# A two-layer hybrid encoder on one core: the rotary key's column tile with low parts in its second half

## Chip, cores and metric

The kernel runs on 1 core of a Trainium2 chip. The metric is the device time of one execution in microseconds (us). Before the change it is 918.32 us, the median of 3 runs (918.1 to 919.2).

## What is computed

Two encoder layers over 256 positions of 1024 features. Each layer normalizes x, makes one combined projection, runs three mixing branches, merges them through gates, and then runs a SwiGLU block and an embedding block. The change is in the combined projection; the rest is cut.

```python
h = rms_norm(x, norm_mix_pre[i])
z = h @ w_in[i]
c_q, c_kv, k_rope, q_c, k_c, v_c, g_a, g_b, g_c = jnp.split(z, split_points, axis=-1)
o_a = mla_attention(c_q, c_kv, k_rope, positions, ...)   # k_r = apply_rope(k_rope, positions), 32 columns, all heads
o_b = fourier_mix(h)
o_c = windowed_gqa(q_c, k_c, v_c, positions, gqa_sink[i])
```

## The kernel before

**Products.** Features lie on partitions, the 256 positions along the free axis. All weights come as tiles of 128 by 128, eight to a chunk, 279 chunks in the order of use. SyncE loads a chunk (512 KB) into one of three staging buffers `w`. ScalarE writes the rounded high part `wh` (line 175) and VectorE the low part `wl` (w minus wh, line 180), each with three buffers of its own. x is split in the same way into `XH` and `XL`. A product of a weight tile and an x tile is then three matmuls of 256 columns on TensorE: high by high, low by high, high by low.

**Order.** The program is written out by a planner (class `Order`) with a clock of its own: each part is a generator that is resumed when the planner thinks its inputs are ready. The orders of TensorE, ScalarE and VectorE are exactly the orders in which the planner issues; GpSimd and SyncE are ordered by the framework. So a change of the planner's clock at one place moves instructions on three engines behind it. Each engine works strictly in its order and waits at the first instruction whose inputs are late.

**The first projection of a layer** (`k_outer`, lines 371 to 395, called at line 893). Four pairs of column tiles `z1` are accumulated at once: three query latents, the key latent, the rotary key, the window keys, the window values and the first window queries. For each of the first six contraction tiles k (one chunk each) there are three passes of eight matmuls, all on line 385: `wh` by XH, `wl` by XH, `wh` by XL. The last two contraction tiles (`LATE`) come pair by pair through `mains` (lines 357, 358 and 364). In layer 0 this loop is interleaved with the norm of x: VectorE sums squares into `acc_npre_first`, TensorE reduces them over partitions (`ss_pre_first`, line 486), VectorE makes the mean (`ms_pre_first`), GpSimd the power of minus one half (`rt_pre_first`, line 497), and TensorE spreads it to rows (`pr_pre_first`, line 503).

**The rotary key** is the tile `kr`, column pair 2, column 0. Its 128 columns are the 32 rope columns, the same 32 with halves swapped, and both once more. After the projection the result `zk` is scaled by the norm (line 285), multiplied with cosines and sines `KC`, and one f32 matmul with the constant `sel` (line 844, `pkL`) adds row m and row 32+m and repeats the sum over 128 partitions.

**GpSimd** fills constants, computes the position differences `di` (two int32 subtractions, line 682, for the distance table that VectorE starts at line 687 with `df`), the small powers, and two sums of squares for the latents (line 824).

**After the projection**: `zq12` and `zq3` (window queries), the latents' norm (`ss_lat`, `ms_lat`, `rt_lat`, `pr_lat`), scores of the first window head `sc`, and the Fourier products `pu`, which multiply with a table `dft` split into `mixH` and `mixL` in the same tile as other operands.

Of the kernel before, what the change touches and what calls it, by code (L numbers as in the profile page):

```python
# [9 lines left out]
F32 = mybir.dt.float32  # L10
# [7 lines left out]
P = 128  # L18
# [8 lines left out]
KT = D_MODEL // P  # L27
# [4 lines left out]
T_MM = 0.109  # L32
# [9 lines left out]
LATE = (2, 2, 2)  # L42
CT = 8
# [30 lines left out]
def r128(k):  # L74
    return np.arange(k * P, (k + 1) * P)
# [146 lines left out]
def encoder(ctx: ExitStack, tc: tile.TileContext, order, gxT, pT, pos, cst, dftT, mask, sink, wts, outT):  # L222
    nc = tc.nc
    V, S, G, T = nc.vector, nc.scalar, nc.gpsimd, nc.tensor

    one = ctx.enter_context(tc.tile_pool(name="one", bufs=1))
# [16 lines left out]
    O = Order()  # L243
# [8 lines left out]
    def take(tag, name, shape=(P, 2, SEQ), dt=None):  # L252
        pool, n, d = pools[tag]
        while min(slots[tag]) > O.now:
            yield min(min(slots[tag]), O.now + 0.2)
        q = min(range(n), key=lambda q: slots[tag][q])
        slots[tag][q] = 1e9
        t = pool.tile(list(shape), dt or d, tag=tag, name=name, bufs=n)
        held.append((t, tag, q))
        return t  # L260
# [7 lines left out]
    def line(gen):  # L268

        try:  # L270
            while True:
                O.wait(next(gen))
        except StopIteration as e:
            return e.value
# [33 lines left out]
    def have(key):  # L308

        O.until(lambda: key in rd)  # L310
        O.wait(rd[key])

    ws = Weights(nc, O, stage, high, wts, order)
# [12 lines left out]
    def weights(n=1):  # L326
        O.until(lambda: ws.ready(n) < 1e8)
        O.wait(ws.ready(n))

    def step():  # L330
        ws.flush()
        O.step()

    def mains(ps, keys, rhs, start=True, stop=True, skip=False, there=None):

        i = 0
        while i < len(keys):
            O.until(lambda: ws.ready(high=True) < 1e8)
            O.wait(ws.ready(high=True))
            c, pos = divmod(len(order), CT)  # L340
            group = range(i, min(i + CT - pos, len(keys)))
            w = {}
            ws.use(c, 1)
            for j in group:
                if there and there(j):
                    have(there(j))

            c1, pos = divmod(len(order), CT)
            if c1 != c:
                ws.use(c, -1)  # L350
                continue
            group = range(i, min(i + CT - pos, len(keys)))
            for j in group:
                w[j] = ws.get(keys[j])
            for j in group:
                rh, rl = rhs(j)
                T.matmul(ps, w[j][0], rh, start=start and j == 0, stop=False, skip_group_check=skip)  # L357
                T.matmul(ps, w[j][0], rl, start=False, stop=False, skip_group_check=skip)  # L358
                O.spend(2 * T_MM)
                step()  # L360
            O.until(lambda: ws.at[c] < 1e8)
            O.wait(ws.at[c])
            for j in group:
                T.matmul(ps, w[j][1], rhs(j)[0], start=False, stop=stop and j == len(keys) - 1, skip_group_check=skip)  # L364
                O.spend(T_MM)
                O.step()
            ws.use(c, -1)
            step()
            i = group[-1] + 1

    def k_outer(pairs, key, rhs, done, late):


        for k in range(KT - late):
            have(("x", k))
            if k == 0:
                weights(2 * len(pairs))
                keep_warm(None)
            weights(2 * len(pairs))
            w = [[ws.get(key(k, n, c)) for c in range(2)] for n in range(len(pairs))]  # L380
            xh, xl = rhs(k)
            for part, mov in ((0, xh), (1, xh), (0, xl)):
                for n in range(len(pairs)):
                    for c in range(2):
                        T.matmul(pairs[n][:, c, :], w[n][c][part], mov, start=(k == 0 and c == 0 and part == 0 and mov is xh),  # L385
                                 stop=False, skip_group_check=True)
                        O.spend(T_MM)
                    if n % 3 == 2:
                        O.step()
            ws.flush()  # L390
        for n in range(len(pairs)):
            ks = range(KT - late, KT)
            for c in range(2):
                mains(pairs[n][:, c, :], [key(k, n, c) for k in ks], lambda q: rhs(ks[q]), start=False, skip=True,
                      there=lambda q: ("x", ks[q]))
            done(n)

    zeros = one.tile([P, SEQ], BF16, tag="zeros", name="zeros")
# [3 lines left out]
    def keep_warm(step):  # L402

        if step is None:
            O.warm = None
            return
        pw = ppo.tile([P, SEQ], F32, tag="po", name=f"warm{O.now:.0f}", bufs=1)
        idle[0] = 0.0

        def warm(us):  # L410
            idle[0] += us
            while idle[0] > step:
                idle[0] -= step
                T.matmul(pw, zeros[:, :P], zeros, start=True, stop=True)

        O.warm = warm
# [1 line left out]

    gx = one.tile([P, C_ALL + KT * SEQ], F32, tag="gx", name="gx")
    gs, x = gx[:, :C_ALL], gx[:, C_ALL:].rearrange("p (j t) -> p j t", t=SEQ)  # L420
    ones = one.tile([P, P], F32, tag="ones", name="ones")
    G.memset(ones, 1.0)
    mhalf = one.tile([P, 4], F32, tag="mhalf", name="mhalf")
    G.memset(mhalf, -0.5)
# [304 lines left out]
    def win(i, k, cols):  # L729
        return ("w_in", i, r128(k), cols)  # L730
# [20 lines left out]
    for i in range(DEPTH):  # L751
# [16 lines left out]
        g1 = [[cq[0], cq[1]], [cq[2], cq[3]], [kr, kc_cols], [vc_cols, qc_cols[0]]]  # L768
        z1 = [line(take("mm" if n < 3 else "s", f"z1{L}_{n}")) for n in range(4)]
# [114 lines left out]
        def fourier_tables():  # L884
            for n, at in enumerate((OC + 2, OA, OA + 2)):
# [4 lines left out]
                rd["dft", n] = yield from split_to(at, 2, f)  # L890
                drop(f, rd["dft", n])

        k_outer(z1, lambda k, n, c: win(i, k, g1[n][c]), xr, lambda n: None, LATE[0])
        O.start(latents())
        O.start(fourier_tables())
        O.start(window_vq0(z1[3]))
# [436 lines left out]

        first = [line(take("mm" if q < 3 else "s", f"ff{L}_{q}")) for q in range(4)]
        k_outer(first, lambda k, n, c: (wgu[c], i, r128(k), r128(n)), xr, lambda n: O.start(swiglu(first[n], n)), LATE[1])
        for j in range(4, FT):
            ps = line(take("mm" if j % 2 else "s", f"ff{L}_{j}"))
# [36 lines left out]

        pg = [line(take("mm", f"pg{L}_{q}")) for q in range(3)]
        k_outer(pg, lambda k, n, c: ("w_ple_gate", i, r128(k), r128(2 * n + c)), xr, lambda n: O.start(gated(pg[n], n)), LATE[2])
        last = i == DEPTH - 1
        for c in range(2):
# [80 lines left out]
```

## Time and profile before

| | |
|---|---|
| median of 3 runs | 918.32 us (918.1 to 919.2) |
| the profiled execution | 919.09 us |
| its span in the trace | 917.2 us |
| TensorE busy, matmuls | 897.5 us (98%), 7497 |
| VectorE, ScalarE busy | 690.5 us (75%), 546.9 us (60%) |
| GpSimd busy, instructions | 34.5 us (4%), 50 |
| chain that ended last | TensorE 90%, issue 4%, VectorE 2%, GpSimd 2% |

The span runs from the first to the last instruction in the trace; 1.9 us of the execution lie around it. A matmul's busy time is longer than the distance to the next one, as matmuls are pipelined: the distance is what a matmul costs when many follow each other.

### The profile page before, as it was taken

How to read it: one execution, taken by the hardware profiler on the slowest of the kernel's cores; microseconds unless marked ns; L12 is line 12 of the kernel's file. 1: busy time of each engine (PE TensorE's matmuls, PEld its weight loads, DVE VectorE, ACT ScalarE, POOL GpSimd, SP SyncE). 2: the span in 40 equal slices, each digit the busy share in tenths (PEclk: the TensorE clock that was granted, in tenths of full speed). 3: DMA queues.
4: the chain of work that ended last, by engine and by line, in shares of the span. 5: the costliest groups of instructions: out<-in, count | busy, mean ns of one | idle time of the engine just before them, and what ended most of it. 6: DMA issues, size and time to landing. Idle time of an engine off the chain costs nothing.

```text
span 917.2 us, 18357 instructions
## 1 busy us (share of the span) xinstructions
PE 897.5 (98%) x7497; PEld 890.2 (97%) x7497; DVE 690.5 (75%) x1066; ACT 546.9 (60%) x937; POOL 34.5 (4%) x50
## 2 busy tenths in 40 slices
PE   8999999999999999999999999999999999999995
PEld 7999999999999999999999999999999999999995
DVE  6899888786887777445789998887858877764475
ACT  6688667645654445444657786776556545544444
POOL 2200000000000000000002000000000000000001
PEclk9999999999999999999999999999999999999998
DMA  7632544555556556554554344544655566555551
GB/s 255 188 123 82 172 160 139 165 173 182 169 168 211 185 185 185 184 184 138 171 156 145 105 138 133 178 157 146 199 178 171 179 190 188 187 174 177 184 163 69
DMA packets 43845, 152.25 MB, mean 166 GB/s; under 512 B 5232, under 2 KB 6000, under 8 KB 43760
## 3 DMA queue, kind: packets, MB, share of 16 engines
q1 hardware_dynamic: 43760, 151.07, 52.3%
q8 instruction: 59, 0.97, 0.4%
q14 instruction: 26, 0.21, 0.1%
HBM read 150.00 MB, written 1.05 MB: 165 GB/s over the span
## 4 chain that ended last, share of the span: by engine, by line
PE 90%; issue 4%; DVE 2%; POOL 2%; DMA 1%; ACT 0%; SPq 0%; DVEq 0%; POOLq 0%; ACTq 0%
PE ffL L364 8%; PE ffL L358 8%; PE ffL L357 8%; PE gpL L364 5%; PE ofL L364 5%; PE ofL L358 5%; PE ofL L357 5%; PE gpL L358 5%; PE gpL L357 5%; PE ffL L385 4%; PE brL L364 3%; PE brL L358 3%; PE brL L357 3%; PE z1L L385 2%; PE omL L364 2%
## 5 line engine op out<-in xcount | busy, mean ns | idle before, releaser
L180 DVE TENSOR_TENSOR wl<-w,wh 128x1024 fp32r<-128x1024 f32 (+1 forms) x280 | 339.9, 1218 | 92.1 <-ACT wh L175 91.5
L175 ACT ACTIVATE wh<-w 128x1024 fp32r<-128x1024 f32 (+1 forms) x280 | 293.8, 1054 | 192.8 <-PE ofL L358 49.6
L357 PE MATMUL ffL<-xs_mixL,wh 128*128 128x256 f32 x608 | 148.4, 281 | 0.0
L358 PE MATMUL ffL<-xs_mixL,wh 128*128 128x256 f32 x608 | 148.2, 281 | 0.0
L357 PEld LDWEIGHTS ffL<-xs_mixL,wh 128*128 128x128 f32 x608 | 114.7, 189 | 0.0
L358 PEld LDWEIGHTS ffL<-xs_mixL,wh 128*128 128x128 f32 x608 | 114.7, 189 | 0.0
L358 PE MATMUL ofL<-hidL,wh 128*128 128x256 f32 x352 | 87.0, 283 | 0.0
L357 PE MATMUL ofL<-hidH,wh 128*128 128x256 f32 x352 | 87.0, 283 | 0.0
L364 PE MATMUL ffL<-xs_mixL,wl 128*128 128x256 f32 x608 | 86.6, 281 | 0.0
L364 PEld LDWEIGHTS ffL<-xs_mixL,wl 128*128 128x128 f32 x608 | 78.3, 189 | 0.0
L358 PEld LDWEIGHTS ofL<-hidL,wh 128*128 128x128 f32 x352 | 67.0, 190 | 0.0
L357 PEld LDWEIGHTS ofL<-hidH,wh 128*128 128x128 f32 x352 | 67.0, 190 | 0.0
L357 PE MATMUL brL<-mixH,wh 128*128 128x256 f32 x256 | 64.1, 283 | 0.0
L358 PE MATMUL brL<-mixL,wh 128*128 128x256 f32 x256 | 64.0, 283 | 0.0
L285 DVE TENSOR_TENSOR fzL<-ffL,R_pre_mixL 128x512 f32<-128x512 f32 x44 | 30.0, 689 | 32.8 <-PE ffL L364 32.5
L364 PE MATMUL ofL<-hidH,wl 128*128 128x256 f32 x352 | 52.2, 284 | 0.0
L358 PEld LDWEIGHTS brL<-mixL,wh 128*128 128x128 f32 x256 | 49.0, 191 | 0.0
L357 PEld LDWEIGHTS brL<-mixH,wh 128*128 128x128 f32 x256 | 49.0, 191 | 0.0
L357 PE MATMUL gpL<-xs_pleL,wh 128*128 128x256 f32 x192 | 48.3, 284 | 0.0
L357 PE MATMUL gpL<-xs_first,wh 128*128 128x256 f32 x192 | 48.0, 283 | 0.0
L358 PE MATMUL gpL<-xs_pleL,wh 128*128 128x256 f32 x192 | 47.7, 281 | 0.0
L358 PE MATMUL gpL<-xs_first,wh 128*128 128x256 f32 x192 | 47.4, 280 | 0.0
(429 smaller groups left out, 2030.1 us busy)
## 6 DMA issues: line engine op xcount, KB each, us to landing
w<-wts SPq DMA_DIRECT2D x278, 512.0 KB, 3.5
dftL<-dft SPq DMA_DIRECT2D x6, 256.0 KB, 3.9
gx<-gx SPq DMA_DIRECT2D x3, 256.0 KB, 5.5
outT<-gx SPq DMA_DIRECT2D x3, 256.0 KB, 2.3
w<-wts SPq DMA_DIRECT2D x2, 256.0 KB, 3.3
p<-pT SPq DMA_DIRECT2D x2, 256.0 KB, 3.8
dist<-mask SPq DMA_DIRECT2D x1, 256.0 KB, 6.4
outT<-gx SPq DMA_DIRECT2D x2, 128.0 KB, 2.4
```

The costliest lines, as they stand in the source:

```text
L175: self.nc.scalar.activation(h[:, s], w[:, s], AF.Copy)
L180: self.nc.vector.tensor_tensor(out=l[:, s], in0=w[:, s], in1=h[:, s], op=ALU.subtract)
L285: V.tensor_tensor(out=out, in0=a, in1=b, op=op)
L357: T.matmul(ps, w[j][0], rh, start=start and j == 0, stop=False, skip_group_check=skip)
L358: T.matmul(ps, w[j][0], rl, start=False, stop=False, skip_group_check=skip)
L364: T.matmul(ps, w[j][1], rhs(j)[0], start=False, stop=stop and j == len(keys) - 1, skip_group_check=skip)
L385: T.matmul(pairs[n][:, c, :], w[n][c][part], mov, start=(k == 0 and c == 0 and part == 0 and mov is xh), stop=False, skip_group_check=True)
```

## The change

The second half of the rotary key's high tile, columns 64 to 127, is overwritten by a GpSimd copy with the low parts of the same weights (the two halves held the same columns). One matmul of that tile by XH then gives high by high in rows 0 to 63 and low by high in rows 64 to 127; one by XL adds high by low (and low by low). So the tile takes two matmuls for a contraction tile in place of three, 16 fewer in all. The constant `sel` now adds four rows, m, 32+m, 64+m and 96+m. The two matmuls stand in the third pass; in the late part the tile's four matmuls come behind those of the window keys. The copies are 8 a layer, each behind the split of its chunk. The constant `ones` shrinks from 128 columns to 1.

```diff
--- before.py
+++ after.py
@@ -368,7 +368,12 @@
             step()
             i = group[-1] + 1
 
-    def k_outer(pairs, key, rhs, done, late):
+    def beside(w):
+
+        G.tensor_copy(w[0][:, 64:], w[1][:, 64:])
+        O.run("pool", 0.3)
+
+    def k_outer(pairs, key, rhs, done, late, twin=None):
 
 
         for k in range(KT - late):
@@ -378,11 +383,19 @@
                 keep_warm(None)
             weights(2 * len(pairs))
             w = [[ws.get(key(k, n, c)) for c in range(2)] for n in range(len(pairs))]
+            if twin:
+                beside(w[twin[0]][twin[1]])
             xh, xl = rhs(k)
-            for part, mov in ((0, xh), (1, xh), (0, xl)):
+            for q, (part, mov) in enumerate(((0, xh), (1, xh), (0, xl))):
                 for n in range(len(pairs)):
                     for c in range(2):
-                        T.matmul(pairs[n][:, c, :], w[n][c][part], mov, start=(k == 0 and c == 0 and part == 0 and mov is xh),
+                        if (n, c) == twin:
+                            if q == 2:
+                                for m in (xh, xl):
+                                    T.matmul(pairs[n][:, c, :], w[n][c][0], m, start=False, stop=False, skip_group_check=True)
+                                    O.spend(T_MM)
+                            continue
+                        T.matmul(pairs[n][:, c, :], w[n][c][part], mov, start=(k == 0 and q == 0 and c == (twin == (n, 0))),
                                  stop=False, skip_group_check=True)
                         O.spend(T_MM)
                     if n % 3 == 2:
@@ -390,9 +403,26 @@
             ws.flush()
         for n in range(len(pairs)):
             ks = range(KT - late, KT)
+            tw = []
+            if twin and twin[0] == n:
+                ws.align(2)
+                weights(late)
+                ws.use(len(order) // CT, 1)
+                at = len(order) // CT
+                tw = [ws.get(key(k, *twin)) for k in ks]
+                for w in tw:
+                    beside(w)
             for c in range(2):
-                mains(pairs[n][:, c, :], [key(k, n, c) for k in ks], lambda q: rhs(ks[q]), start=False, skip=True,
-                      there=lambda q: ("x", ks[q]))
+                if not (tw and c == twin[1]):
+                    mains(pairs[n][:, c, :], [key(k, n, c) for k in ks], lambda q: rhs(ks[q]), start=False, skip=True,
+                          there=lambda q: ("x", ks[q]))
+            for k, w in zip(ks, tw):
+                have(("x", k))
+                for q, m in enumerate(rhs(k)):
+                    T.matmul(pairs[n][:, twin[1], :], w[0], m, start=False, stop=(q == 1 and k == KT - 1), skip_group_check=True)
+                    O.spend(T_MM)
+            if tw:
+                ws.use(at, -1)
             done(n)
 
     zeros = one.tile([P, SEQ], BF16, tag="zeros", name="zeros")
@@ -418,7 +448,7 @@
 
     gx = one.tile([P, C_ALL + KT * SEQ], F32, tag="gx", name="gx")
     gs, x = gx[:, :C_ALL], gx[:, C_ALL:].rearrange("p (j t) -> p j t", t=SEQ)
-    ones = one.tile([P, P], F32, tag="ones", name="ones")
+    ones = one.tile([P, 1], F32, tag="ones", name="ones")
     G.memset(ones, 1.0)
     mhalf = one.tile([P, 4], F32, tag="mhalf", name="mhalf")
     G.memset(mhalf, -0.5)
@@ -890,7 +920,7 @@
                 rd["dft", n] = yield from split_to(at, 2, f)
                 drop(f, rd["dft", n])
 
-        k_outer(z1, lambda k, n, c: win(i, k, g1[n][c]), xr, lambda n: None, LATE[0])
+        k_outer(z1, lambda k, n, c: win(i, k, g1[n][c]), xr, lambda n: None, LATE[0], (2, 0))
         O.start(latents())
         O.start(fourier_tables())
         O.start(window_vq0(z1[3]))
@@ -1403,8 +1433,7 @@
     cst = np.zeros((P, 2 * P), np.float32)
     cst[:, :P] = np.eye(P, dtype=np.float32)
     for m in range(P):
-        cst[m % 32, P + m] = 1.0
-        cst[32 + m % 32, P + m] = 1.0
+        cst[m % 32::32, P + m] = 1.0
     gns = np.zeros((P, C_ALL), np.float32)
     far = np.abs(np.arange(SEQ)[:, None] - np.arange(SEQ)[None, :]) > WINDOW
     mask = np.ascontiguousarray(np.where(far, np.float32(1e30), np.float32(0)).reshape(2, P, SEQ).transpose(1, 0, 2))
```

**GpSimd, the head of the program** (`wh<-wl` are the new copies, `ISA` is the instruction that stands ahead of `di`). Before:

```order
L1108 MEMSET altL_619 128x512
L682 ISA
L682 TENSOR_TENSOR di<-posr,posc 128x256 x2
L497 TENSOR_TENSOR rt_pre_first<-ms_pre_first,mhalf 128x2
L824 TENSOR_TENSOR s01L_479<-s01L_479 128x256
L824 TENSOR_TENSOR s01L_479<-s01L_479,s23L_480 128x256
L497 TENSOR_TENSOR rt_latL_611<-ms_latL_608,mhalf 128x4
```

Now:

```order
L1138 MEMSET altL_618 128x512
L373 COPY wh_123<-wl_124 128x64
L373 COPY wh_125<-wl_126 128x64
L373 COPY wh_127<-wl_128 128x64
L373 COPY wh_251<-wl_252 128x64
L712 ISA
L712 TENSOR_TENSOR di<-posr,posc 128x256 x2
L373 COPY wh_284<-wl_285 128x64
L527 TENSOR_TENSOR rt_pre_first<-ms_pre_first,mhalf 128x2
L373 COPY wh_323<-wl_324 128x64
L373 COPY wh_401<-wl_402 128x64 x2
L854 TENSOR_TENSOR s01L_476<-s01L_476 128x256
```

Four copies, for contraction tiles 0 to 3, now stand ahead of the ISA instruction and of `di`, the fifth stands behind `di`, the sixth behind `rt_pre_first`.

**TensorE, layer 0, contraction tiles 4 and 5** (`wh_284` and `wl_285` are tile 4, `wh_323` and `wl_324` tile 5). Before:

```order
L385 MATMUL z1L_1_137<-xs_first,wh_284 128x256 x2
L385 MATMUL z1L_2_138<-xs_first,wh_284 128x256 x2
L385 MATMUL z1L_3_139<-xs_first,wh_284 128x256 x2
L385 MATMUL z1L_0_136<-xs_first,wh_323 128x256 x2
L385 MATMUL z1L_1_137<-xs_first,wh_323 128x256 x2
L385 MATMUL z1L_2_138<-xs_first,wh_323 128x256 x2
L385 MATMUL z1L_3_139<-xs_first,wh_323 128x256 x2
L385 MATMUL z1L_0_136<-xs_first,wl_324 128x256 x2
L385 MATMUL z1L_1_137<-xs_first,wl_324 128x256 x2
L385 MATMUL z1L_2_138<-xs_first,wl_324 128x256 x2
L503 MATMUL pr_pre_first<-cs,rt_pre_first 128x128 x2
```

Now:

```order
L516 MATMUL ss_pre_first<-ones,acc_npre_first 128x1 x2
L398 MATMUL z1L_3_139<-xs_first,wl_285 128x256 x2
L398 MATMUL z1L_0_136<-xs_first,wh_284 128x256 x2
L398 MATMUL z1L_1_137<-xs_first,wh_284 128x256 x2
L395 MATMUL z1L_2_138<-xs_first,wh_284 128x256 x2
L398 MATMUL z1L_2_138<-xs_first,wh_284 128x256
L398 MATMUL z1L_3_139<-xs_first,wh_284 128x256 x2
L533 MATMUL pr_pre_first<-cs,rt_pre_first 128x128 x2
L398 MATMUL z1L_0_136<-xs_first,wh_323 128x256 x2
L398 MATMUL z1L_1_137<-xs_first,wh_323 128x256 x2
```

The spreading of the norm, `pr_pre_first`, moved from the second pass of tile 5 to the end of tile 4; the pair of line 395 is the rotary key's.

**VectorE, layer 0, behind the projection** (`ms_lat` is the latents' mean, `mixL<-dftL_0` the low part of the first Fourier table, `zq` the window queries). Before:

```order
L293 TENSOR_SCALAR ms_latL_608<-ss_latL_603 128x2 x2
L285 TENSOR_TENSOR mixL_135<-dftL_0_483,mixH_134 128x512
L180 TENSOR_TENSOR wl_573<-w_472,wh_572 128x1024
L285 TENSOR_TENSOR qcL_140<-zqL_567,qcL_140 64x512 x2
L289 SCALAR_TENSOR_TENSOR zqL_635<-zq3L_569,R_pre_first 128x256
L289 SCALAR_TENSOR_TENSOR sbcL_0_648<-dist,scL_0_625 128x512
```

Now:

```order
L293 TENSOR_SCALAR ms_latL_559<-ss_latL_554 128x2 x2
L285 TENSOR_TENSOR zvsL_529<-z1L_3_139,R_pre_first 128x256
L289 SCALAR_TENSOR_TENSOR zq0L_568<-z1L_3_139,R_pre_first 128x256
L753 TENSOR_SCALAR TT<-KC 64x256 x2
L289 SCALAR_TENSOR_TENSOR zqL_588<-zq12L_482,R_pre_first 128x512
L180 TENSOR_TENSOR wl_575<-w_467,wh_574 128x1024
L285 TENSOR_TENSOR qcL_140<-zq0L_568,qcL_140 64x256 x2
L285 TENSOR_TENSOR vcL_144<-vctL_581,vcL_144 128x2x128
L285 TENSOR_TENSOR qcL_140<-zqL_588,qcL_140 64x512 x2
L289 SCALAR_TENSOR_TENSOR zqL_627<-zq3L_571,R_pre_first 128x256
L285 TENSOR_TENSOR mixL_135<-dftL_0_480,mixH_134 128x512
L289 SCALAR_TENSOR_TENSOR sbcL_0_642<-dist,scL_0_637 128x512
```

Between `ms_lat` and the table's low part there now stand nine entries, twelve instructions, that were elsewhere before. On TensorE `ss_lat` stood behind 50 matmuls of `zq12` and `zq3`'s first 22; it now stands behind 44 of `zq12`, and from it to the second matmul of `pu` there are 4 of `zq12`, 24 of `zq3`, 2 transposes, 4 of `pr_lat`, 4 of `sc` and 2 of `pu`.

## Rows read from the trace of the kernel before

**Rows 1.** The page: busy us, share of the span and instructions of each engine.
```profile
PE 897.5 (98%) x7497; PEld 890.2 (97%) x7497; DVE 690.5 (75%) x1066; ACT 546.9 (60%) x937; POOL 34.5 (4%) x50
```

**Rows 2.** Timeline of TensorE, 0 to 48 us: start, us, instruction, count, idle before.
```profile
1.09 3.75 PE L414 MATMUL warm<-zeros 128*128 128x256 bf16 x18 [1.09 <-POOL zeros L399]
...
20.65 0.58 PE L486 MATMUL ss_pre_first<-ones,acc_npre_first 128*128 128x1 f32 x4 [0.32 <-DVE acc_npre_first L285]
...
24.99 0.71 PE L503 MATMUL pr_pre_first<-cs,rt_pre_first 128*128 128x128 f32 x4 [0.84 <-POOL rt_pre_first L497]
...
32.34 0.28 PE L357 MATMUL zq12L<-xs_first,wh 128*128 128x256 f32 x1
...
40.84 0.50 PE L486 MATMUL ss_latL<-ones,s01L 128*128 128x1 f32 x4
...
42.83 0.39 PE L318 MATMUL puL<-mixL,xs_first 128*128 128x256 f32 x1
...
43.70 1.16 PE L503 MATMUL pr_latL<-cs,rt_latL 128*128 128x128 f32 x8 [0.38 <-POOL rt_latL L497]
```

**Rows 3.** Timeline of VectorE, 0 to 48 us.
```profile
14.26 1.38 DVE L180 TENSOR_TENSOR wl<-w,wh 128x1024 fp32r<-128x1024 f32 x1 [0.17 <-ACT wh L175]
...
19.75 0.42 DVE L687 CAST df<-di 128x512 f32<-128x512 int32 x1
20.08 0.42 DVE L285 TENSOR_TENSOR acc_npre_first<-acc_npre_first 128x256 f32<-128x256 f32 x1
...
22.16 0.15 DVE L293 TENSOR_SCALAR ms_pre_first<-ss_pre_first 128x2 f32<-128x2 f32 x1
...
35.76 1.13 DVE L723 TENSOR_SCALAR TT<-KC 64x256 f32<-64x256 f32 x2
36.92 1.22 DVE L180 TENSOR_TENSOR wl<-w,wh 128x1024 fp32r<-128x1024 f32 x1
38.17 0.87 DVE L285 TENSOR_TENSOR qcL<-zq0L,qcL 64x256 fp32r<-64x256 f32 x2
...
41.82 0.23 DVE L293 TENSOR_SCALAR ms_latL<-ss_latL 128x2 f32<-128x2 f32 x2 [0.94 <-PE ss_latL L486]
42.08 0.69 DVE L285 TENSOR_TENSOR mixL<-dftL,mixH 128x512 fp32r<-128x512 f32 x1
...
43.94 1.41 DVE L285 TENSOR_TENSOR qcL<-zqL,qcL 64x512 fp32r<-64x512 f32 x2
```

**Rows 4.** Timeline of GpSimd, whole span.
```profile
2.35 0.52 POOL L1108 MEMSET altL<- 128x512 f32 x1
13.70 2.42 POOL L682 TENSOR_TENSOR di<-posr,posc 128x256 int32<-128x256 int32 x2 [10.83 <-DMA posc<-pos]
22.45 2.48 POOL L497 TENSOR_TENSOR rt_pre_first<-ms_pre_first,mhalf 128x2 f32<-128x2 f32 x1 [6.34 <-DVE ms_pre_first L293]
...
478.68 1.64 POOL L497 TENSOR_TENSOR rt_pre_pleL<-ms_pre_pleL,mhalf 128x2 f32<-128x2 f32 x1 [21.64 <-DVE ms_pre_pleL L293]
```

**Rows 5.** Timeline of TensorE, layer 1's first projection and its latents' norm.
```profile
460.98 2.06 PE L385 MATMUL z1L<-xs_pleL,wh 128*128 128x256 f32 x16
...
475.22 1.11 PE L385 MATMUL z1L<-xs_pleL,wh 128*128 128x256 f32 x8
...
491.94 1.16 PE L503 MATMUL pr_latL<-cs,rt_latL 128*128 128x128 f32 x8 [1.01 <-POOL rt_latL L497]
```

**Rows 6.** Source view of line 682, the position differences on GpSimd.
```profile
L682 POOLq MODIFY_POOL_CONFIG  x2: 4/4/4, 2.8 to 2.9; - x2
...
  DMA posc<-pos: 10.8, 1
```

**Rows 7.** DMA issues: us from issue to landing at the end.
```profile
posc<-pos SPq DMA_DIRECT2D x1, 1.0 KB, 5.7
snk<-sink SPq DMA_DIRECT2D x1, 8.0 KB, 6.4
```

**Rows 8.** One stretch: length, busy us by engine, then granted clock, DMA share, GB/s.
```profile
910.00:918.00 8.00, 0.00 (x0) 0.00 (x0) 2.36 (x4) 0.00 (x0) 1.77 (x2) 0.50 0.36 133
```

## The prediction

> **What bounds the kernel now.** I read the page's busy line first. TensorE works 98% of the span, VectorE 75%, GpSimd 4% [rows 1]. So a matmul taken away pays its distance to the next one, unless TensorE then waits for something, and an engine with 4% of work can cost time only by standing in the way of TensorE. That distance is read in layer 1, where matmuls follow without a gap: 120 of them start between 460.98 and 475.22 [rows 5], 14.24 / 120 = 0.1187 us each.
>
> The timeline of TensorE over the first 48 us comes second, since layer 0's head is where it does wait: 0.32 us at `ss_pre_first` (20.65, for the sums of squares), 0.84 us at `pr_pre_first` (24.99, for GpSimd's power), 0.38 us at `pr_lat` (43.70) [rows 2]. The third view is VectorE's timeline, to see what sets 20.65: the conversion `df` of the position differences at 19.75, and right behind it the last addition of the sums of squares, 20.08 + 0.42 [rows 3]. VectorE keeps its order, so whoever delays `df` delays that addition, and with it TensorE. `df` reads `di` from GpSimd, and the fourth view is GpSimd's timeline: its two subtractions run from 13.70 to 16.12, after 10.83 us of waiting for the positions [rows 4]. They are 3.6 us early.
>
> The fifth view is the source view of the subtractions' line. The ISA instruction ahead of them is two MODIFY_POOL_CONFIG, which take 4 ns each at 2.8 to 2.9 us, right behind the fill that ends at 2.87 [rows 4, 6]. Any work that they start has from 2.9 to 13.7 us to pass unseen in the wait for the positions. The trace of before can't tell how much of these 10.8 us it uses.
>
> **The change, part by part.** A measurement of this kernel can tell about 0.2% (1.84 us) from no change. The profiled execution took 919.09 us, 0.77 above the median of 918.32; the terms below are differences, so I add them to the profiled time and then take the 0.77 off.
>
> *Layer 1's eight matmuls.* The rotary key's tile saves one matmul per contraction tile, and TensorE never waits in this stretch [rows 5]: 8 x 0.1187 = 0.95 us less. The copies are off the path: 64 columns each, for which the fill of 512 columns in 0.52 us [rows 4] is an upper bound, behind a split that comes a pass or more before the third pass needs it. Without that cover each would cost up to 0.52 us. **-0.95.**
>
> *The configuration on GpSimd.* This is the largest term. The order shows four copies ahead of the ISA instruction. GpSimd keeps its order, so it configures only after the copy for contraction tile 3, and that waits for VectorE's split of tile 3, which runs from 14.26 to 15.64 [rows 3]. With some 0.3 us for the copy, that is 16.0. The configuration then has no wait to hide in. Its price is in no row. From below it is nothing: its two instructions take 4 ns, and it might start no work. From above it is the 10.83 us in which it is hidden now. Between the two stand the rows that are nearest in kind, transfers of little data in the same stretch, 5.7 us for 1 KB and 6.4 us for 8 KB [rows 7]. I take the longer, since a load of code is no smaller: 22.4. The subtractions took 2.42 us beside VectorE's work; VectorE will stand still now, and `rt_pre`, the same instruction in two places, took 2.48 in the one and 1.64 in the other [rows 4], so I take 1.7: `di` is ready at 24.1 and `df` starts at 24.2 in place of 19.75. **+4.45**; the ends are 0 (16.0 + 2.42 is still before 19.75) and 16.0 + 10.85 + 1.7 + 0.1 - 19.75 = 8.9. VectorE waits in `df` all this time with the last addition and the split of tile 5 behind it, and TensorE waits in `ss_pre_first`. The matmuls saved for tiles 0 to 4 in layer 0 only make it arrive earlier at that wait: they count nothing. The copy of tile 4, behind `di`, is done by 24.5 and needed after TensorE's release at 25.1.
>
> The Trainium skill ("GPSIMD Engine Reference", section on instruction dispatch) says that the first call to a freshly loaded GpSimd kernel pays about 6 us with no visible instruction. By that figure `df` would start at 23.8 and the term be +4.05 (an estimate from that page), the total 923.5; no run here shows it yet.
>
> *The rest of the head.* From `ss_pre_first` to the first `zq12` matmul it was 32.34 - 20.65 = 11.69 us [rows 2]. Now `ms_pre_first` stands ahead of the split of tile 5 (before, it started at 22.16, behind the split at 21.02): 0.6 us after the start of `ss`, `rt` 0.3 later as before (22.16 to 22.45), `rt` itself 1.64 [rows 3, 4]. So `pr` starts at +2.6, takes 0.46 and 0.1 for its release, and behind it come 23 matmuls of tile 5 and 46 of the late part, 69 x 0.1187 = 8.19. Sum 11.35: **-0.34**. The other end is that `rt` waits behind the split of tile 6, about +1.7.
>
> *Behind the projection.* The second `pu` matmul reads the Fourier table's low part, `mixL`. Before, VectorE made it right behind `ms_lat` (41.82, then 42.08) [rows 3]. Now nine entries stand between. From rows of the same shapes [rows 3]: two of 256 columns (0.42 each), the two of `TT` 1.13, one of 512 columns 0.69, a split 1.22, `qc` 0.87, 0.42, `qc` 1.41, 0.42, and then `mixL` 0.69, together 7.69 less 0.08 of overlap at each of ten, 6.9. With 0.25 for `ms_lat` the table is ready 7.1 us after `ss_lat` ends. TensorE reaches it after 28 matmuls of `zq` (3.32), the transposes (0.25), `pr_lat` (0.9), four of `sc` and one of `pu` (0.6), about 5.1. It waits 2.0 us. The wait of 0.38 at `pr_lat` [rows 2] goes, as 3.6 us of matmuls now stand ahead of it. **+1.6**, with ends 0 (the planner's table runs ahead of what I add up, or the matmuls of the other pair fill in) and 2.5 (a transpose waits too).
>
> *The clock.* After TensorE's last work the granted clock stands at 0.50, the 1.2 GHz level [rows 8], and in the head 18 matmuls from a cold start took 3.75 us, 0.208 each [rows 2], against 0.1187. A wait of 4.5 us may bring the lower level on. If it lasts for as many matmuls again it costs 18 x 0.089 = 1.6, of which the 11 that stand ahead of `pr` lie in a wait of 0.85 anyway. **+0.8**, ends 0 and 1.6.
>
> *`ones` and `sel`* change no instruction count: nothing.
>
> Sum: -0.95 + 4.45 - 0.34 + 1.6 + 0.8 = +5.56. Profiled 924.65, **median 923.9**.
>
> **The rivals.** *The configuration costs nothing in its new place.* For it: two instructions of 4 ns, and no wait that the trace of before charges to them. Against it: a configuration that starts no work would hardly be issued, and the 10.8 us behind it would hide anything. Then `df` is in time, TensorE never cools, and -0.95 - 0.34 + 1.6 = +0.3 is left: 918.6. Chance 0.13.
>
> *Faster.* The mechanism is the same with a second condition: the configuration is free, and VectorE's entries ahead of the table run while TensorE is still at `zq`, so that there is no stall at `pu`, and in both layers the waits for `pr_lat`, 0.38 and 1.01 [rows 2, 5], are covered by matmuls. It gives -0.95 - 0.34 - 1.39 = -2.68: 915.6. It decides where the load costs under 2.0 us (16.0 + 2.0 + 1.7 = 19.7, the time of `df` now) and the table is ready 5.1 us after `ss_lat`. For it: the late place of `ss_lat`. Against it: the 7.1 us added up above. Chance 0.05.
>
> *A new wait at the power.* The configuration is free, but `rt_pre_first` runs beside or behind the split of tile 6 and adds the 1.7 named above to the 0.3: 920.3, slower than can be overlooked by a little. Chance 0.04. That the change doesn't do what it says falls out: 16 matmuls are gone in the order.
>
> **How the numbers follow.** The forecast, slower by a late `di`, has 0.78: it needs the load to cost over 3.5 us or so, and the nearest rows lie above that. Its own range is 921.0 (a load of 4.3 us makes the term 2.35, and no cold clock) to 929.5 (the upper end 8.9 alone gives 928.3, with the upper ends of the last two terms 930.0). For 8 in 10 I go down to the first rival, 918.2, and leave out the faster one: 918.2 to 929.5. Faster by over 0.2%: 0.05; within 0.2%: 0.13, the first rival; slower: 0.78 + 0.04 = 0.82.
>
> **What would show it.** In the new profile: MODIFY_POOL_CONFIG at about 16 us in place of 2.8; `di` starting near 22.4 behind an idle GpSimd; `df` at 24.2 with VectorE idle for some 5 us before it; TensorE waiting over 4 us at `ss_pre_first`; the granted clock at 0.50 in the stretch after it; `zq12` at about 37; a wait of 2 us at the second `pu`; 7481 matmuls; layer 1's projection 0.95 us shorter. If `di` starts at 16.1 the forecast is wrong and the first two rivals are left. If layer 1 saves nothing, a copy is late there, and my cover for it was wrong.

## The result

The changed kernel takes 925.82 us (median of 6 runs, 924.65 to 928.18), beside 918.37 us for the kernel before. The ratio is 1.0083, with a 95% interval of 1.0068 to 1.0098: 7.45 us slower, between 6.2 and 9.0. The forecast was 923.9. It had the side right, and most of its reason wrong.

The profiled execution is the longest of the six (928.18 us, span 926.4), so its rows add up to some 2 us more than the median does. The page after:

```profile
span 926.4 us, 18349 instructions
...
PE 899.7 (97%) x7481; PEld 890.1 (96%) x7481; DVE 691.4 (75%) x1066; ACT 547.6 (59%) x937; POOL 41.7 (4%) x66
```

The 16 matmuls are gone (7481 for 7497 in [rows 1]), GpSimd has its 16 copies. The timeline of GpSimd after and the source view of the line of `di` answer to [rows 4, 6]:

```profile
16.73 0.64 POOL L373 CAST wh<-wl 128x64 fp32r<-128x64 f32 x1 [2.36 <-DVE wl L180]
17.41 2.16 POOL L712 TENSOR_TENSOR di<-posr,posc 128x256 int32<-128x256 int32 x2
19.52 0.70 POOL L373 CAST wh<-wl 128x64 fp32r<-128x64 f32 x1
23.06 1.64 POOL L527 TENSOR_TENSOR rt_pre_first<-ms_pre_first,mhalf 128x2 f32<-128x2 f32 x1 [2.85 <-DVE ms_pre_first L293]
```

```profile
L712 POOLq MODIFY_POOL_CONFIG  x2: 8/8/8, 17.3 to 17.3; - x2
```

The configuration did move behind the fourth copy, to 17.3 us. But `di` starts 0.1 us behind it and is done at 17.41 + 2.16 = 19.57. Nothing is loaded that anyone waits for. VectorE's `df` starts at 20.05 instead of 19.75, with no idle time before it:

```profile
20.05 0.45 DVE L717 CAST df<-di 128x512 f32<-128x512 int32 x1
```

The largest term of the forecast isn't there.

Where the time goes is seen in the timeline of TensorE, at a few landmarks. Before, layer 0's stretch from the first `zq12` (32.34, [rows 2]) to the first `omL` matmul, and layer 1's projection and what follows:

```profile
206.81 0.28 PE L357 MATMUL omL<-mgL,wh 128*128 128x256 f32 x1
...
459.00 0.48 PE L385 MATMUL z1L<-xs_pleL,wh 128*128 128x256 f32 x2 [0.21 <-DVE xs_pleL L289]
...
483.28 0.28 PE L357 MATMUL zq12L<-xs_pleL,wh 128*128 128x256 f32 x1
...
657.87 0.28 PE L357 MATMUL omL<-mgL,wh 128*128 128x256 f32 x1
```

And after:

```profile
10.70 1.10 PE L398 MATMUL z1L<-xs_first,wh 128*128 128x256 f32 x7 [1.64 <-ACT wh L175]
...
22.29 0.50 PE L516 MATMUL ss_pre_first<-ones,acc_npre_first 128*128 128x1 f32 x4
...
33.50 0.28 PE L357 MATMUL zq12L<-xs_first,wh 128*128 128x256 f32 x1
...
44.58 1.13 PE L533 MATMUL pr_latL<-cs,rt_latL 128*128 128x128 f32 x8 [1.26 <-DVE vcL L285]
...
46.97 0.39 PE L318 MATMUL puL<-mixL,xs_first 128*128 128x256 f32 x1 [0.68 <-DVE mixL L285]
...
216.31 0.28 PE L357 MATMUL omL<-mgL,wh 128*128 128x256 f32 x1
...
468.24 0.35 PE L398 MATMUL z1L<-xs_pleL,wh 128*128 128x256 f32 x1 [0.21 <-DVE xs_pleL L289]
...
491.50 0.28 PE L357 MATMUL zq12L<-xs_pleL,wh 128*128 128x256 f32 x1
...
667.68 0.28 PE L357 MATMUL omL<-mgL,wh 128*128 128x256 f32 x1
```

The difference at a landmark (after less before) is +1.16 us at the first `zq12`, +9.50 at `omL`, +9.24 at layer 1's first `z1`, +8.22 at its `zq12`, +9.81 at its `omL`. So layer 0's mixing stage loses 9.50 - 1.16 = 8.34 us, layer 1's projection wins 1.02 and its mixing stage gives 1.59 back. The sums of TensorE's waits in the stretch of layer 0 (`zq12` to `omL`), before and then after, columns: waiting instruction, whom it waits for, us in total, times, longest:

```profile
PE pr_latL L503 <- POOL rt_latL L497: 0.4, 1, 0.4
```

```profile
PE gpL L364 <- DVE wl L180: 1.5, 3, 0.8
PE ptaL0h L958 <- DVE plaL0h L285: 1.4, 1, 1.4
PE pr_latL L533 <- DVE vcL L285: 1.3, 1, 1.3
PE pabL L317 <- DVE UL L289: 0.8, 1, 0.8
PE puL L318 <- DVE mixL L285: 0.7, 1, 0.7
PE ptcL L958 <- ACT sbcL L281: 0.6, 1, 0.6
PE ptcL L958 <- DVE plcL L285: 0.5, 1, 0.5
PE poL0c L982 <- DVE oL0c L285: 0.2, 1, 0.2
```

That is 7.0 us in ten waits, where there was 0.4 in one. A wait costs more than the idle time shown: a matmul's busy time is 0.28, its distance to the next 0.12, so behind a wait 0.16 comes on top (an estimate from these two figures), 1.4 for nine waits more. 6.6 + 1.4 = 8.0 of the 8.34. All but one are waits for VectorE, each for another instruction: not one late operand, but orders of VectorE and TensorE that no longer fit each other.

### The profile page after: what moved, and what is told of

Its sections match the earlier page's. It is cut to its first block, busy times and chain, and to the rows that moved or that the text cites. A ratio compares the mean times of both kernels' runs of the same rounds, so it can differ in the third digit from the quotient of the medians.

```text
span 926.4 us, 18349 instructions
## 1 busy us (share of the span) xinstructions
PE 899.7 (97%) x7481; PEld 890.1 (96%) x7481; DVE 691.4 (75%) x1066; ACT 547.6 (59%) x937; POOL 41.7 (4%) x66
## 4 chain that ended last, share of the span: by engine, by line
PE 85%; DVE 5%; issue 4%; ACT 2%; DMA 2%; POOL 1%; SPq 0%; DVEq 0%; ACTq 0%; POOLq 0%
PE ffL L364 8%; PE ffL L358 8%; PE ffL L357 8%; PE ofL L364 5%; PE ofL L358 5%; PE ofL L357 5%; PE gpL L364 4%; PE gpL L357 4%; PE gpL L358 4%; PE ffL L398 4%; PE brL L364 3%; PE z1L L398 3%; PE brL L358 3%; PE brL L357 3%; PE omL L364 2%
```

## Experiments

Theory O says that this new order is the loss, and that the twin (the name for the copies and two products) is harmless. Theory C blames the copies, theory H the slower head. The first four runs tell them apart; in all of them the kernel before took 917.66 us on the same chip.

**The twin in the old order.** The planner is charged as if nothing had changed: one product's time in each of the three passes, two and one in the late part, and no time on GpSimd. In the late part the two copies stand where the third products stood, and the four matmuls come behind the tile's other column, as in the changed kernel.

```diff
-        O.run("pool", 0.3)
...
                         if (n, c) == twin:
                             if q == 2:
                                 for m in (xh, xl):
                                     T.matmul(pairs[n][:, c, :], w[n][c][0], m, start=False, stop=False, skip_group_check=True)
-                                    O.spend(T_MM)
+                            O.spend(T_MM)
                             continue
...
             for j in group:
-                T.matmul(ps, w[j][1], rhs(j)[0], start=False, stop=stop and j == len(keys) - 1, skip_group_check=skip)
+                if twin is not None:
+                    beside(w[j])
+                    twin.append((c, j, w[j]))
+                    ws.use(c, 1)
+                else:
+                    T.matmul(ps, w[j][1], rhs(j)[0], start=False, stop=stop and j == len(keys) - 1, skip_group_check=skip)
                 O.spend(T_MM)
...
```

> The twin of both layers (copies, two products, 16 matmuls fewer), with the planner's clock charged as before the change, so that the orders of VectorE, ScalarE and SyncE are those of the kernel before, row for row, and TensorE's but for the twin's own matmuls. Theory O (the loss is the new order behind the projection: the changed profile has 7.13 us of waits on TensorE between the first zq12 matmul and 193 us, where before has 0.61): 0.95 us less in layer 1, and in layer 0 between nothing and 0.95, as waits take part of it: 916.5 to 917.5. Theory C (the copies cost: GpSimd's queue, the shared port, late high tiles): over 918.4, up to 925.8. Theory H (the slower head, +1.16 us at the first zq12 matmul with a granted clock of 0.57, comes from the copies or from the two-product pass): 917.7 to 918.5.

Measured: 915.82 us, ratio 0.9979 (0.9970 to 0.9988), 1.84 us faster than before, and 0.7 under the range of theory O. This is the version that beats both. Its TensorE, the landmarks and the waits of layer 0's stretch:

```profile
20.83 0.61 PE L510 MATMUL ss_pre_first<-ones,acc_npre_first 128*128 128x1 f32 x4
...
31.30 0.28 PE L358 MATMUL zq12L<-xs_first,wh 128*128 128x256 f32 x1
...
205.71 0.28 PE L358 MATMUL omL<-mgL,wh 128*128 128x256 f32 x1
...
456.46 1.06 PE L403 MATMUL z1L<-xs_pleL,wh 128*128 128x256 f32 x7 [0.21 <-DVE xs_pleL L289]
...
480.19 0.28 PE L358 MATMUL zq12L<-xs_pleL,wh 128*128 128x256 f32 x1
```

```profile
PE pr_latL L527 <- POOL rt_latL L521: 0.4, 1, 0.4
```

From `zq12` to `omL` it takes 174.41 us, before 174.47: the stretch is back to the old one, with its single wait. The first `zq12` comes 1.04 us earlier than before, of which nothing was won up to `ss_pre_first` (20.83 for 20.65) and all of it behind. Layer 1's projection takes 23.73 us for 24.28: it wins 0.55 and not 0.95, as the wait for GpSimd's power in it is 0.67 us long for 0.30. The profile's span is 3.5 us shorter than before, about twice the gain in medians: 1.4 of it lie between `omL` and layer 1's `z1`, where nothing was changed, so for the gain as a whole the medians are the measure. Theory O stands; all 16 copies and the two-product passes are in this kernel, so theories C and H fall as causes of the loss.

**The new order with three products.** The changed kernel's order, the copies gone, the products back, `sel` as it was.

```diff
-                                for m in (xh, xl):
-                                    T.matmul(pairs[n][:, c, :], w[n][c][0], m, start=False, stop=False, skip_group_check=True)
-                                    O.spend(T_MM)
+                                for h, m in ((0, xh), (0, xl), (1, xh)):
+                                    T.matmul(pairs[n][:, c, :], w[n][c][h], m, start=False, stop=False, skip_group_check=True)
+                                O.spend(2 * T_MM)
...
```

> No twin: three products for the rotary key's tile and no copies, but in the changed kernel's order (VectorE, ScalarE and SyncE row for row, the 16 matmuls back on TensorE behind the twin's place). Theory O: the loss stays and the 16 matmuls come on top, 0.95 us in layer 1 and 0 to 0.95 in layer 0: 926.5 to 927.8. Theory C: the loss goes with the copies, 918 to 919. Theory H: between, some 1.2 us under theory O: 925.3 to 926.6.

Measured: 927.24 us, ratio 1.0102 (1.0085 to 1.0119), 9.58 us slower. The whole loss is there without a copy and without one saved matmul.

**No copies.**

```diff
     def beside(w):
-
-        G.tensor_copy(w[0][:, 64:], w[1][:, 64:])
         O.run("pool", 0.3)
```

> The changed kernel without its 16 GpSimd copies; the second half of the rotary key's high tile keeps the repeated high parts, so its low parts are left out and those columns are counted twice. Every order but GpSimd's is that of the changed kernel. Theory O: the same as the changed kernel within 0.5 us, 925.3 to 926.3. Theory C: 917.0 to 918.4. Theory H: 1.2 us less than the changed kernel, 924.6.

Measured: 925.17 us, ratio 1.0085 (1.0071 to 1.0099). The changed kernel's ratio was 1.0083: the copies cost nothing that can be measured. In us it is 0.1 under the range of theory O and 0.6 over the figure of theory H, which this run alone couldn't exclude. Against the run with three products it is 2.07 us less for 16 matmuls, 0.13 each, near the distance of 0.1187 in the trace, though each of the two ratios is uncertain by over 0.1%.

**Layer 1 alone.** Layer 0 keeps three products, so its planner keeps its clock.

```diff
-            T.matmul(pk, sel, krot, start=True, stop=True)
+            r = P if i else 64
+            T.matmul(pk, sel[:r], krot[:r], start=True, stop=True)
...
-        k_outer(z1, lambda k, n, c: win(i, k, g1[n][c]), xr, lambda n: None, LATE[0], (2, 0))
+        k_outer(z1, lambda k, n, c: win(i, k, g1[n][c]), xr, lambda n: None, LATE[0], (2, 0) if i else None)
```

> The twin in layer 1 alone; layer 0 has its three products and its order of before (its sum over the rotary rows reads the first 64 rows). Theory O: layer 0 costs what it did; in the changed profile layer 1 won 1.02 us in its projection, and behind it gave back 1.35, so 918.7, with an uncertainty of 0.8. If the gain of layer 1's projection is kept: 917.4. Theory C with half of the copies: 920 to 922.

Measured: 917.47 us, ratio 1.0000 (0.9990 to 1.0010). In medians it is 0.19 us under the kernel before, nearer to 917.4 than to 918.7. The interval, 0.9 us to either side of the kernel before, is 916.7 to 918.6: it holds 917.4 and ends just under 918.7, which was itself given with an uncertainty of 0.8. The waits in its layer 1, 484 to 672 us:

```profile
PE pr_latL L533 <- POOL rt_latL L527: 1.0, 1, 1.0
PE gpL L364 <- DVE wl L180: 0.3, 1, 0.3
PE brL L358 <- DVE mixL L285: 0.3, 1, 0.3
PE ptcL L959 <- DVE plcL L285: 0.2, 1, 0.2
```

The last three aren't in the kernel before, whose only wait in that stretch is that for `pr_lat`, 1.0. So layer 1 too gives some of its gain back by a new order, a small part of what layer 0 loses; how much exactly, the medians leave open.

**Moving the planner's clock alone.** If the order is all, the kernel before must become slow without any change of its work. Three kernels have one line more behind layer 0's projection, a fourth has it in the changed kernel. Theory S says that any shift costs, since the planner's constants were chosen for one clock; theory P that the cost grows with the shift; theory T that only the twin's own order costs. The kernel before took 918.44 us beside them.

```diff
         k_outer(z1, lambda k, n, c: win(i, k, g1[n][c]), xr, lambda n: None, LATE[0])
+        O.spend(-0.872 if i == 0 else 0.0)
```

> The kernel before, with no twin, and its planner's clock set back by 0.872 us once, behind layer 0's first projection: as much as the 8 saved matmuls take off the planner's clock. No work is added or removed; only orders behind that place move (194 lines of difference on VectorE, 162 on ScalarE). Theory S (the loss is that the planner's constants were tuned to one clock, and any shift costs): 3 to 9 us more than before, 921 to 927. Theory T (the twin's own order in the projection is what costs, its late part and its place for the copies): within 1 us of before, 917 to 919.

Measured: 925.42 us, ratio 1.0075 (1.0058 to 1.0092).

> The same with 0.218 us, a quarter of that (230 lines on VectorE). Theory S: 1 to 9 us more than before, not in proportion to the shift. A theory P, that the loss grows with the shift: a quarter of what the shift by 0.872 gives. Theory T: within 1 us of before.

Measured: 923.37 us, ratio 1.0060 (1.0039 to 1.0081).

> The same with the clock set forward by 0.218 us (126 lines on VectorE). Theory S: 0 to 5 us more than before, as any shift leaves the tuned order. Theory P: a shift the other way gains, or costs nothing: 917 to 918.4.

Measured: 919.26 us, ratio 1.0005 (0.9993 to 1.0016).

> The changed kernel, its planner's clock set forward by 0.872 us behind layer 0's first projection, so that the planner meets the mixing stage at the time it did before, though with what was started earlier in another order. If the shift at that place is what costs: 916.5 to 918.5. If what costs is the order inside the projection (where the norm's and the latents' parts fell), or any difference at all: 920 to 927.

Measured: 928.41 us, ratio 1.0110 (1.0091 to 1.0129), over both ranges.

The waits of TensorE from 30 to 200 us, of the shifts by -0.872, -0.218 and +0.218 and of the changed kernel with its clock put forward, in this order:

```profile
PE pr_latL L503 <- POOL rt_latL L497: 1.3, 1, 1.3
PE puL L318 <- DVE mixL L285: 1.3, 1, 1.3
PE saL0h L317 <- DVE kpL L285: 0.7, 1, 0.7
...
```

```profile
PE poL0c L953 <- DVE plcL L285: 2.9, 1, 2.9
PE pr_latL L503 <- POOL rt_latL L497: 1.3, 1, 1.3
...
```

```profile
PE gpL L364 <- DVE wl L180: 1.1, 1, 1.1
```

```profile
PE puL L318 <- DVE mixL L285: 4.5, 1, 4.5
PE puL L317 <- ACT mixH L281: 1.3, 1, 1.3
...
```

Each shift gives other waits at other places. But the waits are not the whole price: in the profiles of both shifts back and of the changed kernel with its clock put forward, the granted clock of TensorE falls behind such waits. For the shift by -0.218, the landmarks of layer 0's stretch and two slices of it, and for the shift by -0.872 one slice (columns of a slice: its ends, length, busy us of TensorE, its weight loads, VectorE, ScalarE and GpSimd, granted clock, DMA share, GB/s):

```profile
31.97 0.28 PE L357 MATMUL zq12L<-xs_first,wh 128*128 128x256 f32 x1
...
213.81 0.28 PE L357 MATMUL omL<-mgL,wh 128*128 128x256 f32 x1
```

```profile
44.00:48.00 4.00, 4.00 (x23) 4.00 (x23) 3.84 (x10) 1.06 (x2) 0.00 (x0) 0.57 0.21 66
72.00:76.00 4.00, 4.00 (x24) 4.00 (x24) 2.84 (x9) 1.01 (x3) 0.19 (x1) 0.62 0.00 0
```

```profile
48.00:52.00 4.00, 4.00 (x21) 4.00 (x21) 3.90 (x11) 3.99 (x12) 0.35 (x1) 0.54 0.02 6
```

These slices stand right behind waits, the first two behind those of 1.3 and 2.9 us; in the kernel before the clock is 1.00 there. Where 36 matmuls run in 4 us at 1.00, 21 to 24 ran here, at or near the level of 1.2 GHz. For the shift by -0.218 an estimate from these figures: the waits, 4.5 us in three for 0.4 in one, cost 4.1 + 0.3, the slow slices 25 x 0.1187 = 3.0, together 7.4, and the stretch takes 213.81 - 31.97 = 181.84 us, 7.37 more than before. The whole span is only 4.4 us longer, as this execution was shorter elsewhere. In layer 0's stretch of the changed kernel the clock doesn't fall; its loss there is the waits.

0.218 us less on the planner's clock costs 4.9 us in medians, four times as much shift costs 7.0, and the same shift the other way can't be told from none. A quarter of 7.0 would be a ratio of 1.0019, below the interval of the small shift. So theory P falls, and theory T too: the kernel before loses 7 us with none of the twin in it. Theory S holds in a weaker form: two of the three shifts of the kernel before cost much, the third nothing that can be told. Putting the clock right at the end of the projection doesn't repair the changed kernel, it stays slow at 928.41. By then the order inside the projection differs, and what had been started there has other places; that this is why it stays slow is argued and not shown, and how much of the loss is due to the order inside the projection and how much to the shift behind it, these runs don't tell apart. Of what was tried, only charging each piece as before, at its own time, gave the old order back.

## Why the prediction was right and wrong

*Layer 1's eight matmuls*, -0.95: right. Its projection took 1.02 us less (+9.24 to +8.22), and its copies were in time, though a copy took up to 0.70 us, more than the bound of 0.52 that I had taken from a fill. That 1.59 us come back behind it was not in the sum; the order there was taken as unchanged.

*The configuration on GpSimd*, +4.45: wrong, and this is the step that failed. It moved behind the fourth copy as said (17.3, forecast 16.0), but cost nothing: the lower end of the bounds, where I had taken a value near two small transfers. Those rows are no kin of it; 4 ns of instruction and no wait charged to it in the trace were all that was known. The same 0.1 us between configuration and `di` stands in the trace of the twin in the old order. The Trainium skill ("GPSIMD Engine Reference", section on instruction dispatch) has about 6 us for the first call to a freshly loaded kernel; no such time shows here between 17.3 and 17.41, and the measurement decides. Whether anything was loaded afresh, the trace doesn't say.

*The rest of the head*, -0.34: right in kind. From `ss_pre_first` to `zq12` it is 33.50 - 22.29 = 11.21 us for 11.69, -0.48; in the old order 31.30 - 20.83 = 10.47, -1.22, as `rt` took 0.76 there and TensorE no longer waited for it.

*Behind the projection*, +1.6: right in size. The table's low part is ready 46.24 + 0.68 = 46.92, 7.26 us after `ss_lat` ends (39.66; forecast 7.1). TensorE waits 1.26 + 0.68 = 1.94 us (forecast 2.0), but two thirds of it already at `pr_lat`, for `vcL` (done at 44.42), the move of the transposes out of the accumulator buffer that `pr_lat` takes next; I had given the transposes 0.25 us on TensorE alone: with `pr_lat` gone as a wait for GpSimd, it came back as one for VectorE. The rows of TensorE and VectorE:

```profile
39.08 0.58 PE L516 MATMUL ss_latL<-ones,s23L 128*128 128x1 f32 x4
```

```profile
44.00 0.42 DVE L285 TENSOR_TENSOR vcL<-vctL,vcL 128x256 fp32r<-128x256 f32 x1
...
46.24 0.68 DVE L285 TENSOR_TENSOR mixL<-dftL,mixH 128x512 fp32r<-128x512 f32 x1
```

*The clock*, +0.8: it fell, but elsewhere, as shown in the last section, and not from a wait at `ss_pre_first`.

*What was left out* is larger than all of these. I followed the new order to the second `pu`, at 47 us, and took the rest of the stage as equal. The other eight waits, 7.0 - 1.94 = 5.1 us with another 1.3 behind them, lie between 70 and 154 us. The total came near by luck: a term of +4.45 that isn't there stood in for waits of 5.1 that were not looked for. The first rival, that the configuration costs nothing, was right in its condition and wrong in its time, 918.6, for the same reason.

## What to carry to other kernels

Where a planner with a clock of its own writes the order, the price of a small edit is the whole new order behind it: compare the orders to the end of the stage on every engine that is near full, since a first stall that is costed exactly says nothing of the next eight. A change of work can be tested apart from its order by charging the planner as before; here that turned 7.5 us lost into 1.8 us won. A wait of TensorE can cost more than its length: behind some of those seen here the granted clock fell, to 0.54 to 0.62 in slices of 4 us. And where the trace gives a mechanism no time at all, the nearest rows in kind are no price for it: the forecast should then stand on what can be counted.

## What the hardware showed beyond that

The granted clock fell in the head of the profiled execution of the changed kernel. The columns are those of the slices above:

```profile
8.00:12.00 4.00, 2.20 (x18) 1.79 (x16) 2.37 (x5) 3.20 (x6) 0.04 (x1) 1.00 1.03 403
12.00:16.00 4.00, 4.00 (x21) 4.00 (x22) 3.83 (x7) 3.93 (x7) 0.82 (x2) 0.57 0.86 279
16.00:20.00 4.00, 4.00 (x36) 4.00 (x36) 3.42 (x4) 2.64 (x3) 3.23 (x4) 1.00 0.69 237
```

At 0.57, near the 1.2 GHz level, 21 matmuls ran in 4 us, where 36 run at 1.00: 15 x 0.1187 = 1.8 us lost by this estimate, in an execution that is 2.4 us over its median. It follows TensorE's wait of 1.64 us at 10.70, which is for a weight chunk that landed later than before (0.74 there). The changed kernel with its clock put forward has the same head, and its profile the same fall: 0.57 from 12 to 16 us, behind a wait of 1.83 us at that place. In the run without copies, with the same order, the clock stays at 1.00 and the first `zq12` comes at 32.70, and in the run with three products it stays there too. So the copies may have a part in it, though the medians show no cost of theirs (ratios 1.0083 and 1.0085); this, and what makes the chunk land late, was not tried.
